# Half of x behind the first weights, rstd on the sums, shift in halves: a reordered start of a fused decoder step on one core

## The chip, the cores and the metric

The kernel runs on one core of a Trainium2 chip. Its metric is the device time of one execution in microseconds (us). The engines are named as in the profile: PE is TensorE (PEld its weight loads), DVE is VectorE, ACT is ScalarE, POOL is GpSimd, and SP is the queue that issues most of the transfers.

## The reference

One step of a one-layer hybrid recurrent decoder trunk in fp32, for 256 prompt tokens and 32 sample tokens (8 sequences of 4), D = 2048. What is cut from it here is the inside of the three mixer branches.

```python
def rmsnorm(x, g):
    y = x * rsqrt(mean(x * x, axis=-1) + EPS)
    return y * g
mod = silu(c) @ w_ada + b_ada                    # c: one row for the prompt, 8 for the samples
sh1, sc1, gt1, sh2, sc2, gt2 = split(mod, 6)
xn = rmsnorm(x, g_norm1) * (1.0 + sc1) + sh1
proj = xn @ w_in                                 # lru_x, q, k, v, gates, ...: 13 groups of columns
...                                              # RG-LRU, GLA and mLSTM branches, merge gates
x = x + gt1 * (merged @ w_out)
xn = rmsnorm(x, g_norm2) * (1.0 + sc2) + sh2
x = x + gt2 * (square(relu(xn @ w_ff1)) @ w_ff2)
y = rmsnorm(x, g_final)
```

## The kernel before

All activations lie feature by partition: 16 tiles (KT) of 128 features by N = 288 tokens, of which the first NP = 256 are the prompt's and the last 32 the samples'. A weight matrix is read in blocks of 512 output columns. `stream` takes a block through PE: for each group of two k tiles it loads 512 KB of weights (`raw`), ScalarE rounds them to `hi`, VectorE forms the rest `lo = raw - hi`, and PE adds three products for each of 4 column tiles and 2 k tiles, `hi*xh + hi*xl + lo*xh`: 24 matmuls of 128x288 a group. `raw`, `hi` and `lo` have three buffers each. A block's four sums lie in PSUM (`mm`, four buffers) and are taken out by `evac`.

The modulation rows (SC1, SH1, ...) come from `w_ada`, which is read in tiles of 1 MB ("units"). `load_one` issues the next unit's load into a slot, and `visit` puts the products of the units that are held on PE (`pa`, line 256). Where both happen is written out by hand: `every("L L L L . V")` gives one token for each group of a stream, L for a load, V for a visit, and a dot for nothing. The loads stand in SP's queue in the order of the program, so an L whose slot isn't free holds back the weight loads behind it. A slot comes free by a visit. The order on PE, DVE, ACT and POOL is made by a scheduler, apart from `issue_after`, which puts an instruction behind another on its engine, and `high_priority`.

The first stretch goes as follows. ScalarE's queue loads x in four pieces, 16 squares are summed by PE (`pi`, line 455) and `rstd_of` makes rstd. `drain("sc0")` takes the eight units of the first half of SC1, and `scale1(0)` forms `x * rstd * sc` for k tiles 0 to 7 and splits it into xh and xl (`modulate`, lines 408 to 438). Blocks 0 to 2 of the projection's q, k and v (NPRE = 3) then run over k tiles 0 to 7 without the shift, `to_slot` takes their sums out (line 465); after the other half of SC1 they run over k tiles 8 to 15, and `plus_slot` adds (line 476). What SH1 gives for these three blocks is added later (`shift_product`, "cor"). For all other blocks `whole` puts xh and xl together again on POOL, `shift` adds SH1 and splits once more (lines 427 to 438), and block 3 starts.

At the end the feed-forward blocks leave x2 in 16 tiles; ScalarE scales tiles 0 to 11 by `g_final` as they come, rstd is made, and the last products (lines 1566 and 1570) and the stores follow.

Of the kernel before, what the change touches and what calls it, by code (L numbers as in the profile page):

```python
# [8 lines left out]
F32 = mybir.dt.float32  # L9
# [5 lines left out]
P = 128  # L15
D = 2048
# [36 lines left out]
def trunk(ctx, tc, io):  # L53
# [91 lines left out]
        at["n"] += 1  # L145
        return [weight_tile(n) for n in ("raw", "hi", "lo")]

    def stream(w, blk, act, kt, evac, g0=0, width=512, ahead=True, k0=0, kg=2):

        nm_t = width // P  # L150
        pss = [pm.tile([P, 512], F32, tag="mm", name=nm("mm")) for _ in range(nm_t)]
        for g in range(k0 // kg, kt // kg):
            with tc.high_priority() if ahead else nullcontext():
                raw, hi, lo = (t.rearrange("p (k m) -> p k m", k=kg) for t in weight_tiles())
                Q.dma_start(raw, w[blk, g0 + g].rearrange("p (k m) -> p k m", k=kg))
                pace["hi"] = S.activation(hi, raw, AF.Copy)  # L156
                pace["lo"] = V.tensor_tensor(out=lo, in0=raw, in1=hi.bitcast(F32), op=ALU.subtract)  # L157
            for m in range(nm_t):
                for kk in range(kg):
                    k = kg * g + kk  # L160
                    xh, xl = act(k)
                    ms = slice(m * P, (m + 1) * P)
                    T.matmul(pss[m][:, :N], hi[:, kk, ms], xh, start=k == k0, stop=False)  # L163
                    T.matmul(pss[m][:, :N], hi[:, kk, ms], xl, start=False, stop=False)  # L164
                    pace["last"] = T.matmul(pss[m][:, :N], lo[:, kk, ms], xh, start=False, stop=k == kt - 1)  # L165
# [173 lines left out]
    left = units()  # L339

    def load_one():
        u = next(left, None)
# [12 lines left out]
    def step(cs):  # L355
        for c in cs:
            if c == "L":
                load_one()
            elif c == "V":
                with tc.high_priority(), tc.issue_after(pace["last"].ins):  # L360
                    visit()

    def drain(n):
        while n not in done:
# [5 lines left out]
    def sumsq(ps, x, k, s):  # L370

        if k == 0:
            S.activation(s, x, AF.Square)
            return
        sq = t288()
        S.activation(sq, x, AF.Square)
# [26 lines left out]
    def smp(a):  # L403
        return a[..., NP:N].rearrange("p k (b t) -> p k b t", b=NB)

    def modulate(xg, rs, k0, fk, xh, xl, xr):

        V.tensor_tensor(out=xr, in0=xg, in1=rs.unsqueeze(1).to_broadcast([P, 4, N]), op=ALU.mult)
        bc = [P, 2, NB, TS]
        for j in range(0, 4, 2):  # L410
            r = slice(k0 + j, k0 + j + 2)
            for i in range(j, j + 2):
                V.tensor_scalar(xr[:, i, 0:NP], xr[:, i, 0:NP], mod[:, fk, k0 + i, 0:1], None, ALU.mult)
            xs = smp(xr[:, j:j + 2])
            G.tensor_tensor(out=xs, in0=xs, in1=mod[:, fk, r, 1:9].unsqueeze(3).to_broadcast(bc), op=ALU.mult)
            split(xh[:, r, :], xl[:, r, :], xr[:, j:j + 2])

    def whole(k0, xh, xl, xr):

        G.tensor_tensor(out=xr, in0=xh[:, k0:k0 + 4, :].bitcast(F32), in1=xl[:, k0:k0 + 4, :].bitcast(F32), op=ALU.add)  # L420

    def shift(k0, shk, xh, xl, xr):

        for j in range(0, 4, 2):
            r = slice(k0 + j, k0 + j + 2)
            for i in range(j, j + 2):
                V.tensor_scalar(xr[:, i, 0:NP], xr[:, i, 0:NP], mod[:, shk, k0 + i, 0:1], None, ALU.add)
            xs = smp(xr[:, j:j + 2])
            V.tensor_tensor(out=xs, in0=xs, in1=mod[:, shk, r, 1:9].unsqueeze(3).to_broadcast([P, 2, NB, TS]), op=ALU.add)
            split(xh[:, r, :], xl[:, r, :], xr[:, j:j + 2])  # L430

    def split(dst_h, dst_l, src):
        n = src.shape[1]
        step = 2 if len(src.shape) == 3 else n
# [8 lines left out]

    xa, xb = slot(0), slot(1)
    xin = halves(xa, xb)
    for i in range(4):
        t = (xa, xb)[i // 2]
        S.dma_start(t[:, 4 * (i % 2):4 * (i % 2) + 4, :], io["x"][:, 4 * i:4 * i + 4, :])
    xh = big.tile([P, KT, N], F32R, tag="xh", name="xh1")
    xl = big.tile([P, KT, N], F32R, tag="xl", name="xl1")  # L450
    ps = longp()
    for k in range(KT):
        sq = t288()
        S.activation(sq, xin(k), AF.Square)
        T.matmul(ps[:, :N], ones, sq, start=k == 0, stop=k == KT - 1)
    rs = rstd_of(ps)

    def act1(k):
        return xh[:, k, :], xl[:, k, :]
# [5 lines left out]
            S.copy(dst[:, base + m, :], p)  # L465
        return f


    slots["ids"] = 2, 4, 5, 6, 7, 8, 9, None
    drain("sc0")  # L470
    xs3, xs4 = slot(3), slot(4)
    qk, vv = slot(8), slot(9)

    def plus_slot(dst, base):
        def f(m, p):
            V.tensor_tensor(out=dst[:, base + m, :], in0=dst[:, base + m, :], in1=p, op=ALU.add)
        return f

    def scale1(h):
        t = (xa, xb)[h]  # L480
        for i in range(2):
            with tc.high_priority():
                modulate(t[:, 4 * i:4 * i + 4, :], rs, 8 * h + 4 * i, SC1, xh, xl, (xs3, xs4)[i % 2][:, 0:4, :])


    slots["ids"] = 2, 5, 6, 7, None
    scale1(0)
# [3 lines left out]
    for b in range(NPRE):  # L491
        run(stream(win, B_Q + b, act1, 8, to_slot((qk, vv)[b // 2], 4 * (b % 2))))
    drain("sc")
    scale1(1)
    for b in range(NPRE):
        run(stream(win, B_Q + b, act1, KT, plus_slot((qk, vv)[b // 2], 4 * (b % 2)), k0=8))
    xrs = [(xs3, xs4)[i % 2][:, 4 * (i // 2):4 * (i // 2) + 4, :] for i in range(4)]
    for i in range(4):
        whole(4 * i, xh, xl, xrs[i])
    drain(SH1)  # L500
    with tc.high_priority():
        for i in range(4):
            shift(4 * i, SH1, xh, xl, xrs[i])
# [121 lines left out]

    ylru = []
    hselr = cp.tile([P, 4], F32R, tag="hselr", name="hselr")
    S.activation(hselr, C("hsel"), AF.Copy)
# [33 lines left out]
    every("L L L L . V . .")  # L662
# [370 lines left out]
    every("L L . V . .")  # L1033
    merge(0, ylru, io["wbl"])


# [388 lines left out]

    merge(1, ygla, io["wbg"])
    slots.update(ids=(None, 8), n=0)
    every("L L . . V . .", skip=5)

    mo = slot(3)  # L1430
    for b in range(2):
# [95 lines left out]
    def ff2(hb, h):  # L1527
        for b in range(4):
            def ev(m, p, b=b):
# [10 lines left out]
                    return  # L1540
                resid(x, p, GT2, k)
                sumsq(pss, x, k, ssum)
                if k < 12:
# [7 lines left out]
    for hb in range(8):  # L1551
# [5 lines left out]
            ssum = row("gc")  # L1557
        ff2(hb, h)
        h = hn
    rs = rstd_of(pss)  # L1560
    for i, (a, b) in enumerate(((0, 2), (8, 10), (2, 5), (10, 12), (5, 8), (12, 14), (14, 16))):
        t = x2[a // 8][:, a % 8:(b - 1) % 8 + 1, :]
        with tc.high_priority():
            if b <= 12:
                E = G if a >= 8 else V
                E.tensor_tensor(out=t, in0=t, in1=rs.unsqueeze(1).to_broadcast([P, b - a, N]), op=ALU.mult)
            else:
                for k in range(a, b):
                    x = x2[1][:, k - 8, :]
# [113 lines left out]
```

## Time and profile before

| | us |
|---|---|
| median of 3 runs (1971.32 to 1976.9) | 1974.94 |
| the profiled execution | 1968.77 |
| its span, first to last instruction | 1967.0 |
| PE busy | 1928.3 |
| DVE busy | 1022.5 |
| ACT busy | 818.1 |
| POOL busy | 223.4 |

The mean granted TensorE clock of that execution is 0.993, and 428.99 MB were moved. In the views below a row of the timeline is: start, length, engine, line, operation, output<-input, form, count, and in brackets the idle time of the engine just before and what ended it. A row of grouped instructions is: line, engine, operation, output<-input, form, count, then busy us and mean ns, then the idle time before them. A row of waits is: who waited, for whom, total us, times, longest. Matmuls are pipelined, and one that stands with 0.29 us starts 0.13 us after the one ahead of it.

### The profile page before, as it was taken

Reading aid. Unit: us, or ns where it says so; the run is one execution under the profiler, and the core shown is the slowest. Engines: PE = TensorE matmul, PEld = TensorE weight load, DVE = VectorE, ACT = ScalarE, POOL = GpSimd, SP = SyncE. Lnnn points to the kernel's source line nnn. Section 1 sums busy time; section 2 is a strip of 40 time slices with the busy share of each in tenths; the row PEclk is TensorE's granted clock in tenths of the full one; section 3 lists DMA queues with packets and bytes.
Section 4 is the critical chain, followed back from the end, with each engine's and each line's share of the span. In section 5 each row is a group of like instructions: output and inputs, shape, how many; then the busy total and the mean of one; then the engine's idle time right before and its main releaser. Section 6 shows DMA issues by size and latency. Waiting matters only on the chain.

```text
span 1967.0 us, 35580 instructions
## 1 busy us (share of the span) xinstructions
PE 1928.3 (98%) x14930; PEld 1819.0 (92%) x14930; DVE 1022.5 (52%) x1512; ACT 818.1 (42%) x1161; POOL 223.4 (11%) x293
## 2 busy tenths in 40 slices
PE   6999999999999999999999999999999999999996
PEld 4879888999999999898999899999999999999996
DVE  3453547545674457654445564445444445454565
ACT  3333365535454354433333453443333334343433
POOL 0300100000123010000013330000000000010102
PEclk8999999999999999999999999999999999999998
DMA  9997765636743359866788554644444444444442
GB/s 382 387 346 275 274 238 221 246 130 247 263 166 134 140 184 324 307 251 238 278 318 330 187 212 170 223 159 170 170 164 160 170 161 161 166 171 168 160 172 102
DMA packets 119377, 428.99 MB, mean 218 GB/s; under 512 B 11744, under 2 KB 11904, under 8 KB 119088
## 3 DMA queue, kind: packets, MB, share of 16 engines
q1 hardware_dynamic: 109600, 391.92, 54.5%
q0 software_dynamic: 4576, 16.57, 2.4%
q10 hardware_dynamic: 5040, 18.22, 2.3%
q8 instruction: 117, 1.92, 0.4%
q14 instruction: 44, 0.36, 0.1%
HBM read 409.85 MB, written 16.81 MB: 217 GB/s over the span
## 4 chain that ended last, share of the span: by engine, by line
PE 90%; DMA 4%; DVE 3%; ACT 1%; issue 1%; SPq 0%; DVEq 0%; ACTq 0%
PE mm L163 27%; PE mm L165 27%; PE mm L164 27%; PE pa L256 4%; DMA raw<-win 3%; DVE lo L157 1%; ACT hi L156 1%; DVE s L513 1%; DMA s<-wada 1%; DMA raw<-wbl 1%; PE px L1343 0%; PE px L594 0%; PE pi L1326 0%; DMA raw<-wbm 0%; PE px L864 0%
## 5 line engine op out<-in xcount | busy, mean ns | idle before, releaser
L157 DVE TENSOR_TENSOR lo<-raw,hi 128x1024 fp32r<-128x1024 f32 x448 | 555.1, 1240 | 618.3 <-ACT hi L156 605.0
L156 ACT ACTIVATE hi<-raw 128x1024 fp32r<-128x1024 f32 x448 | 474.5, 1060 | 804.8 <-PE mm L164 530.3
L163 PE MATMUL mm<-xh,hi 128*128 128x288 f32 x2560 | 755.9, 299 | 9.0 <-ACT xh L437 5.4
L164 PE MATMUL mm<-xl,hi 128*128 128x288 f32 x2560 | 752.0, 296 | 0.0
L165 PE MATMUL mm<-xh,lo 128*128 128x288 f32 x2560 | 732.2, 296 | 1.4 <-DVE lo L157 1.3
L163 PEld LDWEIGHTS mm<-xh,hi 128*128 128x128 f32 x2560 | 479.5, 188 | 32.7 <-issue 13.5
L163 PE MATMUL mm<-s,hi 128*128 128x288 f32 x1664 | 490.0, 297 | 1.6 <-ACT s L1004 1.6
L164 PE MATMUL mm<-s,hi 128*128 128x288 f32 x1664 | 487.9, 295 | 0.0
L164 PEld LDWEIGHTS mm<-xl,hi 128*128 128x128 f32 x2560 | 481.9, 188 | 2.1 <-issue 0.5
L165 PEld LDWEIGHTS mm<-xh,lo 128*128 128x128 f32 x2560 | 474.6, 189 | 5.0 <-DVE lo L157 2.7
L165 PE MATMUL mm<-s,lo 128*128 128x288 f32 x1664 | 475.9, 295 | 0.6 <-DVE lo L157 0.6
L163 PEld LDWEIGHTS mm<-s,hi 128*128 128x128 f32 x1664 | 311.9, 188 | 8.2 <-issue 5.2
L164 PEld LDWEIGHTS mm<-s,hi 128*128 128x128 f32 x1664 | 312.5, 188 | 0.3
L165 PEld LDWEIGHTS mm<-s,lo 128*128 128x128 f32 x1664 | 308.3, 188 | 1.2 <-DVE lo L157 1.1
L157 DVE TENSOR_TENSOR lo<-s,hi 128x1024 fp32r<-128x1024 f32 x80 | 98.0, 1225 | 115.2 <-ACT hi L156 115.2
L156 ACT ACTIVATE hi<-s 128x1024 fp32r<-128x1024 f32 x80 | 84.9, 1061 | 143.2 <-PE mm L164 142.5
L1521 POOL TENSOR_TENSOR t<-t 128x288 f32<-128x288 f32 x64 | 60.2, 951 | 643.0 <-ACT t L1520 643.0
L1537 DVE TENSOR_TENSOR s<-s,mm 128x288 f32<-128x288 f32 x96 | 40.3, 451 | 33.8 <-PE mm L165 32.6
L256 PE MATMUL pa<-s,silc 128*32 128x512 f32 (+1 forms) x488 | 53.1, 521 | 4.6 <-DMA s<-wada 4.6
L438 DVE TENSOR_TENSOR s<-t,s 128x288 fp32r<-128x288 f32 x64 | 33.8, 568 | 15.5 <-ACT s L437 15.5
L1024 POOL TENSOR_TENSOR s<-s,t 128x288 f32<-128x288 f32 x16 | 16.5, 1058 | 192.8 <-DVE t L1023 192.8
L437 ACT ACTIVATE s<-t 128x288 fp32r<-128x288 f32 x64 | 28.0, 441 | 24.6 <-POOL t L1521 24.6
(391 smaller groups left out, 1102.1 us busy)
## 6 DMA issues: line engine op xcount, KB each, us to landing
raw<-win SPq DMA_DIRECT2D x192, 512.0 KB, 5.2
raw<-wf SPq DMA_DIRECT2D x176, 512.0 KB, 4.1
s<-wada SPq DMA_DIRECT2D x48, 1024.0 KB, 8.8
s<-wf SPq DMA_DIRECT2D x80, 512.0 KB, 3.2
ag<-wada SPq DMA_DIRECT2D x30, 1024.0 KB, 5.7
raw<-wout SPq DMA_DIRECT2D x32, 512.0 KB, 5.7
st<-wada SPq DMA_DIRECT2D x24, 512.0 KB, 7.1
s<-win SPq DMA_DIRECT2D x13, 768.0 KB, 6.7
```

The source lines that it names most:

```text
L156: pace["hi"] = S.activation(hi, raw, AF.Copy)
L157: pace["lo"] = V.tensor_tensor(out=lo, in0=raw, in1=hi.bitcast(F32), op=ALU.subtract)
L163: T.matmul(pss[m][:, :N], hi[:, kk, ms], xh, start=k == k0, stop=False)
L164: T.matmul(pss[m][:, :N], hi[:, kk, ms], xl, start=False, stop=False)
L165: pace["last"] = T.matmul(pss[m][:, :N], lo[:, kk, ms], xh, start=False, stop=k == kt - 1)
L256: pace["prod"] = T.matmul(ps[32 * j:32 * j + 32, h * w // 4:(h + 1) * w // 4], stat(k), v[:, j], start=k == 0 and h == 0, stop=k == KT - 1 ...
L437: S.activation(dst_h[:, r], src[:, r], AF.Copy)
L438: V.tensor_tensor(out=dst_l[:, r], in0=src[:, r], in1=dst_h[:, r].bitcast(F32), op=ALU.subtract)
L513: V.scalar_tensor_tensor(y[:, m, s:NP], x[:, m, 0:NP - s], w[:, m, j:j + 1], y[:, m, s:NP], ALU.mult, ALU.add)
L1024: (V if br == 1 else G).tensor_tensor(out=a, in0=a, in1=t, op=ALU.add)
L1521: G.tensor_tensor(out=r, in0=r, in1=r, op=ALU.mult)
L1537: V.tensor_tensor(out=a, in0=a, in1=p, op=ALU.add)
```

## The change

- ScalarE's queue loads only the first half of x. The other half goes into SP's queue in two pieces, by a new token X, behind the first weight groups; a new token N squares it on ScalarE and adds it up on VectorE, and one late matmul ends the sum.
- The eight first sums on PE stand one ahead of each of the eight unit products.
- rstd isn't needed at the start any more: `scale` forms `x * sc` for k tiles 0 to 7 and, later, 8 to 15, and `add_slot` multiplies the finished sums of blocks 0 to 2 by rstd on VectorE (`normalise` puts rstd on x itself, for the other blocks). The prompt columns of xh come from ScalarE with a scale, those of xl from one VectorE operation. The first group's matmuls are ordered: all hi*xh, then hi*xl, then lo*xh.
- `whole` and the old `shift` go. SH1 is made in two halves, and `shift` works on x: k tiles 0 to 7 while the three blocks run, 8 to 15 beside block 3.
- The narrow weights (`wn`) get their own buffer instead of one of the three of `raw`, and load earlier.
- Four patterns of visits have their V one group earlier.
- At the end VectorE makes all the last products, in other pieces; ScalarE scales tiles 12 and 13 too.

```diff
     def stream(..., behind=None):
...
-                pace["lo"] = V.tensor_tensor(out=lo, in0=raw, in1=hi.bitcast(F32), op=ALU.subtract)
+                with tc.issue_after(behind.ins) if behind and g == 0 else nullcontext():
+                    pace["lo"] = V.tensor_tensor(out=lo, in0=raw, in1=hi.bitcast(F32), op=ALU.subtract)
...
+            if behind and g == 0:
+                for i in range(3):
+                    for kk in range(kg):
+                        for m in range(nm_t):
+                            with tc.issue_after(pace["last"].ins) if pace["last"] else nullcontext():
+                                part(m, kk, i)
...
         yield from ada_half("sc", SC1, 1)
-        yield from ada(SH1)
+        yield from ada_half("sh0", SH1, 0)
+        yield from ada_half("sh1", SH1, 1)
...
-    for i in range(4):
-        t = (xa, xb)[i // 2]
-        S.dma_start(t[:, 4 * (i % 2):4 * (i % 2) + 4, :], io["x"][:, 4 * i:4 * i + 4, :])
+    for i in range(2):
+        S.dma_start(xa[:, 4 * i:4 * i + 4, :], io["x"][:, 4 * i:4 * i + 4, :])
...
-    for k in range(KT):
-        sq = t288()
-        S.activation(sq, xin(k), AF.Square)
-        T.matmul(ps[:, :N], ones, sq, start=k == 0, stop=k == KT - 1)
-    rs = rstd_of(ps)
...
+    slots.update(ids=(2, 3, 4, 5, 6, 7, None, 9), n=0)
+    for u in range(8):
+        load_one()
+    for u in range(8):
+        sq = t288()
+        S.activation(sq, xin(u), AF.Square)
+        with tc.issue_after(pace["prod"].ins) if u else nullcontext():
+            pace["sum"] = T.matmul(ps[:, :N], ones, sq, start=u == 0, stop=False)
+        with tc.issue_after(pace["sum"].ins):
+            visit(1)
...
+    def samples(x, r, kind, op):
+        xs, h = x[:, :, NP:N], xh[:, r, NP:N]
+        V.tensor_tensor(out=smp(x), in0=smp(x), in1=mod[:, kind, r, 1:9].unsqueeze(3).to_broadcast([P, 2, NB, TS]), op=op)
+        V.tensor_copy(h, xs)
+        return V.tensor_tensor(out=xl[:, r, NP:N], in0=xs, in1=h.bitcast(F32), op=ALU.subtract)
+    def scale(k, order=None):
...
+            then(samples(x, r, SC1, ALU.mult))
+        for i in range(2):
+            f = mod[:, SC1, k + i, 0:1]
...
+                then(S.activation(xh[:, k + i, 0:NP], x[:, i, 0:NP], AF.Copy, scale=f))
...
+                l = then(V.scalar_tensor_tensor(xl[:, k + i, 0:NP], x[:, i, 0:NP], f, xh[:, k + i, 0:NP].bitcast(F32), ALU.mult, ALU.subtract))
+    def normalise(k):
+        x, r = pair_of(k)
+        for i in range(2):
+            V.scalar_tensor_tensor(x[:, i, 0:NP], x[:, i, 0:NP], mod[:, SC1, k + i, 0:1], rs[:, 0:NP], ALU.mult, ALU.mult)
+        V.tensor_tensor(out=x[:, :, NP:N], in0=x[:, :, NP:N], in1=rs[:, NP:N].unsqueeze(1).to_broadcast([P, 2, NS]), op=ALU.mult)
+    def shift(k):
+        x, r = pair_of(k)
+        samples(x, r, SH1, ALU.add)
+        for i in range(2):
+            f = mod[:, SH1, k + i, 0:1]
+            S.activation(xh[:, k + i, 0:NP], x[:, i, 0:NP], AF.Identity, bias=f)
+            V.scalar_tensor_tensor(xl[:, k + i, 0:NP], x[:, i, 0:NP], f, xh[:, k + i, 0:NP].bitcast(F32), ALU.add, ALU.subtract)
-    def plus_slot(dst, base):
+    def add_slot(dst, base):
         def f(m, p):
-            V.tensor_tensor(out=dst[:, base + m, :], in0=dst[:, base + m, :], in1=p, op=ALU.add)
+            d = dst[:, base + m, :]
+            V.tensor_tensor(out=d, in0=d, in1=p, op=ALU.add)
+            V.tensor_tensor(out=d, in0=d, in1=rs, op=ALU.mult)
...
+    def second_half():
+        while len(sums) < 2:
+            yield
+        with tc.issue_after(pace["last"].ins):
+            T.matmul(ps[:, :N], ones, ssq, start=False, stop=True)
+        inv_sqrt(rs, ps[:, :N], bias=eps, scale=1.0 / D)
...
-    every("L LV " * 4 + "L LLV L LV " * 3 + "LV" + " ." * 40)
+    every(". L X L LV LN XL LV LN LV L L L LV L L LLV L L L LV L L LLV")
...
+    pre = beside(second_half())
+    for h in range(2):
+        for b in range(NPRE):
+            ev = (add_slot if h else to_slot)((qk, vv)[b // 2], 4 * (b % 2))
+            run(stream(win, B_Q + b, act1, 8 + 8 * h, ev, k0=8 * h, behind=None if h or b else ready))
+    finish(pre)
     every("L L L L . V")
...
+    rest = beside(last_shifts())
...
+            wn = sp.tile([P, 1028], F32, tag="st", name=nm("st"), bufs=2)[:, 0:512].rearrange("p (k c) -> p k c", k=KT)
+            Q.dma_start(wn, io["wsm"].rearrange("p (k c) -> p k c", k=KT))
...
-    wn = wp.tile([P, 1024], F32, tag="raw", name=nm("raw"), bufs=3)[:, 0:512].rearrange("p (k c) -> p k c", k=KT)
-    Q.dma_start(wn, io["wsm"].rearrange("p (k c) -> p k c", k=KT))
...
-    every("L L L . V . .", skip=6)
+    every("L L L V . . .", skip=6)
     merge(2, yml, io["wbm"])
...
+        for k in range(12, 14):
+            x = x2[1][:, k - 8, :]
+            S.activation(x, x, AF.Copy, scale=Pm("gf")[:, k:k + 1])
...
-    for i, (a, b) in enumerate(((0, 2), (8, 10), (2, 5), (10, 12), (5, 8), (12, 14), (14, 16))):
+    for i, (a, b) in enumerate(((0, 1), (1, 3), (3, 6), (6, 8), (8, 11), (11, 14), (14, 16))):
...
-            if b <= 12:
-                E = G if a >= 8 else V
-                E.tensor_tensor(out=t, in0=t, in1=rs.unsqueeze(1).to_broadcast([P, b - a, N]), op=ALU.mult)
+            if b <= 14:
+                V.tensor_tensor(out=t, in0=t, in1=rs.unsqueeze(1).to_broadcast([P, b - a, N]), op=ALU.mult)
```

Of the four patterns with an earlier V the one ahead of `merge(2, ...)` is shown; the others are those of the gate blocks, of `merge(0, ...)` and of the two `mo` blocks.

More of the change, by code (lines that the diff above doesn't have):

```diff
@@ L146, in weight_tiles, with stream @@
         return [weight_tile(n) for n in ("raw", "hi", "lo")]
-    def stream(w, blk, act, kt, evac, g0=0, width=512, ahead=True, k0=0, kg=2):
+    def stream(w, blk, act, kt, evac, g0=0, width=512, ahead=True, k0=0, kg=2, behind=None):
         nm_t = width // P
@@ L156, in stream, with part @@
                 pace["hi"] = S.activation(hi, raw, AF.Copy)
-                pace["lo"] = V.tensor_tensor(out=lo, in0=raw, in1=hi.bitcast(F32), op=ALU.subtract)
+                with tc.issue_after(behind.ins) if behind and g == 0 else nullcontext():
+                    pace["lo"] = V.tensor_tensor(out=lo, in0=raw, in1=hi.bitcast(F32), op=ALU.subtract)
+            def part(m, kk, i):
+                k = kg * g + kk
+                ps, ms = pss[m][:, :N], slice(m * P, (m + 1) * P)
+                xh, xl = act(k)
+                w, x = ((hi, xh), (hi, xl), (lo, xh))[i]
+                pace["last"] = T.matmul(ps, w[:, kk, ms], x, start=k == k0 and i == 0, stop=k == kt - 1 and i == 2)
+            if behind and g == 0:
[5 more added lines that the diff above has]
+                yield
+                continue
             for m in range(nm_t):
                 for kk in range(kg):
[L160 to L165, printed above, removed]
+                    for i in range(3):
+                        part(m, kk, i)
                 if g == kt // kg - 1:
@@ L339, in trunk @@
     left = units()
+    also = {}
     def load_one():
@@ L361, in step @@
                     visit()
+            elif c in also:
+                also[c]()
     def drain(n):
@@ L404, in smp @@
         return a[..., NP:N].rearrange("p k (b t) -> p k b t", b=NB)
[L406 to L430, printed above, removed]
     def split(dst_h, dst_l, src):
@@ new lines, in trunk, with pair_of, then, now @@
+    qk, vv = slot(8), slot(9)
+    def pair_of(k):
+        t = (xa, xb)[k // 8]
+        return t[:, k % 8:k % 8 + 2, :], slice(k, k + 2)
+    def samples(x, r, kind, op):
[4 more added lines that the diff above has]
+    def scale(k, order=None):
+        def then(i):
+            if order is not None:
+                order[i.ins.engine] = i
+            return i
+        def now(e):
+            return tc.issue_after(order[e].ins) if order and e in order else nullcontext()
+        x, r = pair_of(k)
+        A, W = mybir.EngineType.Activation, mybir.EngineType.DVE
+        with now(W):
+            then(samples(x, r, SC1, ALU.mult))
+        for i in range(2):
+            f = mod[:, SC1, k + i, 0:1]
+            with now(A):
+                then(S.activation(xh[:, k + i, 0:NP], x[:, i, 0:NP], AF.Copy, scale=f))
+            with now(W):
+                l = then(V.scalar_tensor_tensor(xl[:, k + i, 0:NP], x[:, i, 0:NP], f, xh[:, k + i, 0:NP].bitcast(F32), ALU.mult, ALU.subtract))
+        return l
@@ new lines, in more_x, with norm_part @@
+    def more_x():
+        i = len(xs_)
+        xs_.append(Q.dma_start(xb[:, 4 * i:4 * i + 4, :], io["x"][:, 8 + 4 * i:12 + 4 * i, :]))
+    def norm_part():
+        for k in range(4 * len(sums), 4 * len(sums) + 4):
+            if k == 0:
+                with tc.issue_after(pace["hi"].ins):
+                    S.activation(ssq, xb[:, k, :], AF.Square)
+                continue
+            sq = t288()
+            with tc.issue_after(pace["hi"].ins):
+                S.activation(sq, xb[:, k, :], AF.Square)
+            V.tensor_tensor(out=ssq, in0=ssq, in1=sq, op=ALU.add)
+        sums.append(0)
@@ new lines, in second_half @@
+    def second_half():
+        while len(sums) < 2:
+            yield
+        with tc.issue_after(pace["last"].ins):
+            T.matmul(ps[:, :N], ones, ssq, start=False, stop=True)
+        inv_sqrt(rs, ps[:, :N], bias=eps, scale=1.0 / D)
+        while "sc" not in done:
+            yield
+        for k in range(8, KT, 2):
+            scale(k)
+            yield
+        for k in range(0, KT, 2):
+            normalise(k)
+            yield
+        while "sh0" not in done:
+            yield
+        for k in range(0, 8, 2):
+            shift(k)
+            yield
@@ L488, in trunk, with last_shifts @@
+    def last_shifts():
+        for k in range(8, KT, 2):
+            shift(k)
+            if k != 8:
+                yield
+    xs_, sums = [], []
+    ssq, rs = row("rr"), row("lf")
+    also.update(X=more_x, N=norm_part)
+    slots.update(ids=(2, 3, 4, 5, 6, 7, None), n=0)
+    chain = {}
+    with tc.high_priority():
+        ready = scale(0, chain)
+        for k in range(2, 8, 2):
+            scale(k, chain)
     G.tensor_copy(con[:, 0:1], mod[:, SC1, 0, 0:1])
     G.dma_start(con, io["con"])
-    every("L LV " * 4 + "L LLV L LV " * 3 + "LV" + " ." * 40)
@@ L491, in trunk @@
[L491 to L503, printed above, removed]
+    every(". L X L LV LN XL LV LN LV L L L LV L L LLV L L L LV L L LLV")
@@ L627, in trunk @@
     hselr = cp.tile([P, 4], F32R, tag="hselr", name="hselr")
-    S.activation(hselr, C("hsel"), AF.Copy)
+    with tc.issue_after(pace["hi"].ins):
+        S.activation(hselr, C("hsel"), AF.Copy)
     lx = slot(2)
@@ L660, in gate_silu @@
         return f
-    every("L L L L . V . .")
+    every("L L L L V . . .")
     slots.update(ids=(6, 7, "st", None), n=0)
@@ L1032, in trunk @@
     slots.update(ids=(None, 7), n=0)
-    every("L L . V . .")
+    every("L L V . . .")
     merge(0, ylru, io["wbl"])
@@ L1427, in trunk @@
     slots.update(ids=(None, 8), n=0)
-    every("L L . . V . .", skip=5)
+    every("L L . V . . .", skip=5)
     mo = slot(3)
```

16 lines of the change are left out of this document (4 added, 12 removed).

## The prediction

> **What bounds the kernel now.** The page comes first. Its busy table and its slices say which engine has no time left, and where it still has some.
>
> ```profile
> PE 1928.3 (98%) x14930; PEld 1819.0 (92%) x14930; DVE 1022.5 (52%) x1512; ACT 818.1 (42%) x1161; POOL 223.4 (11%) x293
> ...
> PE   6999999999999999999999999999999999999996
> ```
>
> TensorE (PE) is busy for 98% of the 1967.0 us span; only the first and the last slice show holes. So a change of order can win only what PE does not use: 1967.0 - 1928.3 = 38.7 us, plus stretches where PE is busy at a low clock. The waits of PE say who owns the holes (total, times, longest).
>
> ```profile
> PE pi L455 <- ACT t L454: 6.1, 1, 6.1
> PE mm L163 <- ACT xh L437: 5.4, 1, 5.4
> PE pa L256 <- DMA s<-wada: 4.6, 5, 1.5
> PE mm L163 <- DVE s L476: 2.2, 1, 2.2
> ...
> PE mm L163 <- ACT s L1004: 1.6, 1, 1.6
> ```
>
> The next view is busy time by stretch: length, then PE, PEld, DVE, ACT and POOL busy (instructions), TensorE clock, DMA share, GB/s.
>
> ```profile
> 18.00:22.00 4.00, 2.83 (x36) 1.08 (x34) 2.75 (x5) 0.32 (x1) 0.00 (x0) 1.00 1.02 418
> 22.00:26.00 4.00, 1.79 (x16) 0.59 (x16) 1.05 (x1) 0.00 (x0) 0.00 (x0) 0.65 1.03 417
> 26.00:30.00 4.00, 3.20 (x28) 1.19 (x32) 0.00 (x0) 0.00 (x0) 0.00 (x0) 0.50 1.03 422
> 38.00:42.00 4.00, 3.99 (x16) 3.64 (x16) 4.00 (x6) 2.75 (x4) 0.00 (x0) 0.50 1.03 421
> ...
> 46.00:50.00 4.00, 4.00 (x49) 2.91 (x48) 1.46 (x2) 1.10 (x2) 0.00 (x0) 1.00 1.03 419
> 40.00:120.00 80.00, 79.94 (x663) 65.53 (x662) 35.04 (x41) 25.75 (x35) 16.50 (x10) 0.98 1.00 394
> 70.00:80.00 10.00, 10.00 (x95) 8.91 (x93) 5.43 (x14) 4.93 (x9) 1.32 (x4) 1.00 0.88 343
> 1550.00:1600.00 50.00, 50.00 (x378) 50.00 (x377) 24.93 (x32) 16.99 (x16) 0.00 (x0) 1.00 0.50 178
> ```
>
> Two things bind. The transfers run full until 120 us (share 1.00, 394 GB/s). And PE, once it has its operands, takes 50/378 = 0.132 us a matmul, 3.2 us for a weight group of 24; at clock 0.50 it does 16 in 4 us. The start is read in the timeline (start, length, engine, line).
>
> ```profile
> 31.18 1.07 PE L256 MATMUL pa<-s,silc 128*32 128x256 f32 x16 [0.78 <-DMA s<-wada]
> 32.32 0.45 DVE L219 STREAM_TRANSPOSE t<-pa 128x256 f32<-128x256 f32 x1 [9.27 <-PE pa L256]
> 33.47 1.22 DVE L157 TENSOR_TENSOR lo<-raw,hi 128x1024 fp32r<-128x1024 f32 x1 [0.70 <-ACT hi L156]
> 34.62 0.23 DVE L278 TENSOR_TENSOR mod<-t,par 128x72 f32<-128x72 f32 x1
> 34.88 0.23 DVE L281 SCALAR_TENSOR_TENSOR mod<-mod,par 128x72 f32<-128x72 f32 x1
> 37.66 1.33 PE L163 MATMUL mm<-xh,hi 128*128 128x288 f32 x4 [5.40 <-ACT xh L437]
> 47.14 1.07 PE L256 MATMUL pa<-ag,silc 128*32 128x256 f32 x16
> ...
> 141.53 0.29 PE L165 MATMUL mm<-xh,lo 128*128 128x288 f32 x1
> 144.01 0.37 PE L163 MATMUL mm<-xh,hi 128*128 128x288 f32 x1 [2.19 <-DVE s L476]
> ```
>
> The eighth wada tile lands at 31.18, the first weight matmul starts at 37.66, and two groups (48 matmuls) are through at 47.14: 9.5 us where full clock needs 6.4. From there to 141.5 PE does 22 groups and 24 wada products in 94.4 us without a hole: 22 x 3.2 = 70, so a product costs 1.0 us. Then come 2.3 idle us, and block 3 begins at 144.0.
>
> **Term 1: the first weight matmul comes earlier.** On PE, at the very start (pi: sum of squares of x; pa: wada products; mm: weight matmuls), before:
>
> ```order
> L455 MATMUL pi_108<-t_17_142,ones 128x288
> L256 MATMUL pa_166<-s_27_175,silc 32x256 x8
> L455 MATMUL pi_108<-t_18_145,ones 128x288
> L455 MATMUL pi_108<-t_19_148,ones 128x288
> L455 MATMUL pi_108<-t_20_151,ones 128x288
> L455 MATMUL pi_108<-t_21_154,ones 128x288
> L256 MATMUL pa_166<-s_28_185,silc 32x256 x8
> L256 MATMUL pa_166<-s_29_195,silc 32x256 x8
> ```
>
> and in the change:
>
> ```order
> L460 MATMUL pi_106<-t_19_168,ones 128x288
> L269 MATMUL pa_126<-s_10_115,silc 32x256 x8
> L460 MATMUL pi_106<-t_20_179,ones 128x288
> L269 MATMUL pa_126<-s_11_117,silc 32x256 x8
> L460 MATMUL pi_106<-t_21_190,ones 128x288
> L269 MATMUL pa_126<-ag_119,silc 32x256 x8
> L460 MATMUL pi_106<-t_22_201,ones 128x288
> L269 MATMUL pa_126<-s_13_121,silc 32x256 x8
> L165 MATMUL mm_250<-xh_104,hi_255 128x288
> ```
>
> Eight sums are left, one ahead of each product. Half of x (128 x 2304 floats, 1.18 MB) now loads behind the first weights: at 420 GB/s that is 2.8 us, so the eighth tile lands at 28.4 and its product ends at 29.5. On VectorE (DVE), what stands between that product and xh, before:
>
> ```order
> L219 STREAM_TRANSPOSE t_34_245<-pa_166 128x256
> L157 TENSOR_TENSOR lo_283<-raw_281,hi_282 128x1024
> L278 TENSOR_TENSOR mod<-t_34_245,par 128x72
> L281 SCALAR_TENSOR_TENSOR mod<-mod,par 128x72
> L413 TENSOR_SCALAR s_35_249<-s_35_249,mod 128x256
> ```
>
> and in the change:
>
> ```order
> L232 STREAM_TRANSPOSE t_23_212<-pa_126 128x256
> L291 TENSOR_TENSOR mod<-t_23_212,par 128x72
> L294 SCALAR_TENSOR_TENSOR mod<-mod,par 128x72
> L472 TENSOR_TENSOR s_3_100<-s_3_100,mod 128x2x32
> L473 CAST xh_104<-s_3_100 128x2x32
> L474 TENSOR_TENSOR xl_105<-s_3_100,xh_104 128x2x32
> ```
>
> The lo split has left the path, rstd and its products too; the prompt columns of xh come from ScalarE beside it. The durations of such operations (line, form, count, busy, mean ns):
>
> ```profile
> L429 DVE TENSOR_TENSOR s<-s,mod 128x64 f32<-128x64 f32 x7 | 1.5, 221 | 0.0
> L465 ACT COPY s<-mm 128x288 f32<-128x288 f32 x12 | 4.8, 400 | 16.7 <-PE mm L165 16.1
> L156 ACT ACTIVATE hi<-raw 128x1024 fp32r<-128x1024 f32 x27 | 28.5, 1058 | 59.5 <-DMA raw<-win 45.7 <-PE mm L164 7.1 <-DVE lo L157 3.9
> L476 DVE TENSOR_TENSOR s<-s,mm 128x288 f32<-128x288 f32 x11 | 4.9, 453 | 8.3 <-PE mm L165 7.9
> L157 DVE TENSOR_TENSOR lo<-raw,hi 128x1024 fp32r<-128x1024 f32 x26 | 34.6, 1340 | 34.8 <-ACT hi L156 34.8
> ```
>
> 0.45 + 0.23 + 0.23 + two of 0.22 + gaps of 0.2 = 1.5 us: first matmul at 31.0, 6.7 earlier. ScalarE then has eight scalings queued ahead of the second hi: 8 x 0.40 + 1.06 from 30.6 on ends at 34.9, some 0.7 us after the first group; with the lo behind it I count 1.0 us of stall. At full clock 48 matmuls are through at 31.0 + 6.4 + 1.0 = 38.4 (8.7 gained). At half clock, with 0.7 more for the last product and the old 9.5 us, at 41.2 (5.9 gained). The clock was 1.00 where PE was busy 71% of a stretch (18:22), 0.65 at 45% (22:26), 0.50 later. A sum and a product in each 2.5 us make about 64%, between the first two, so I take the middle: **39.8, a gain of 7.3**. [...]
>
> ```profile
> 26.23 0.20 PEld L256 LDWEIGHTS pa<-s,silc 128*32 128x32 f32 x8 [2.35 <-DMA s<-wada]
> ```
>
> **Term 2: up to block 3.** From 39.8 PE has the same 94.4 us and one late sum (0.55): 134.8. The 2.3 us hole goes, because shift is made by halves: sh0 while groups still run, sh1 behind block 3's first half. What is late next: the splits that VectorE does after each set of products. Behind the sc products the lo of the group after next ends 0.45 + 2 x 0.23 + 6 x 0.22 + 3 x 0.40 + 1.22 = 4.65 us after them, and is wanted a group and 8 matmuls on, at 4.3: 0.35. Behind the sh1 products the next lo ends after 0.45 + 0.23 + 6 x 0.22 + 4 x 0.40 + 1.22 = 4.8: about 0.6. So block 3 starts at **135.7 instead of 144.0: 8.3 us** for terms 1 and 2. rstd costs two adds into one on twelve blocks' sums (12 x 0.45), eight normalisings and a square root inside the stream. They hide under VectorE's idle time (35 busy of 80 us), and the buffer of PSUM comes free after the first add. x's two late loads wait on SP's queue in front of two weight loads; the landings that they wait for are long past.
>
> The cover to watch is the transfers. After the eighth tile 24 groups, 24 tiles and x (12.6 + 25.2 + 1.2 = 39.0 MB) must land before the last four products, at 135.7 - 4 x 1.0 = 131.6. At 394 GB/s they do at 28.4 + 99 = 127.4, 4.2 us early.
>
> **Term 3: visits one group earlier.** The hole behind 144 that this touches, in the timeline: SP stood behind a slot until a visit freed it.
>
> ```profile
> 875.56 0.46 SPq L295 DMA_DIRECT2D s<-wada  x1
> ...
> 891.50 0.33 SPq L155 DMA_DIRECT2D raw<-wbm  x1
> 898.10 0.38 SPq L295 DMA_DIRECT2D ag<-wada  x1
> 906.50 1.06 ACT L156 ACTIVATE hi<-raw 128x1024 fp32r<-128x1024 f32 x1 [8.49 <-DMA raw<-wbm]
> ```
>
> A group (3.2 us) earlier, the 1.6 us wait at 906 goes: **1.5 us**. The last tile of that visit was issued at 875.6, some 20 us before SP went on, so it waits for none. The other patterns meet no wait: nothing. Nor do I count anything for the narrow weights' own buffer.
>
> **Term 4: the end.** VectorE and POOL share the last products; both are slow side by side.
>
> ```profile
> L1566 POOL TENSOR_TENSOR s<-s,row 128x576 f32<-128x576 f32 x2 | 4.1, 2088 | 4.1 <-DVE row L397 4.1
> L1566 DVE TENSOR_TENSOR s<-s,row 128x864 f32<-128x864 f32 x2 | 3.3, 1648 | 0.0
> ...
> 1955.38 2.93 DVE L1566 TENSOR_TENSOR s<-s,row 128x576 f32<-128x576 f32 x2
> ...
> 1959.80 1.04 DVE L1566 TENSOR_TENSOR s<-s,row 128x864 f32<-128x864 f32 x1
> 1960.76 1.36 DVE L1570 SCALAR_TENSOR_TENSOR s<-s,par,row 128x288 f32<-128x288 f32 x3
> ...
> o_y<-s SPq DMA_DIRECT2D x2, 288.0 KB, 2.9
> ```
>
> Alone VectorE took 0.96 for 864 columns (1959.80 to 1960.76) and 0.43 for 288. All of it on VectorE: 0.46 + 3 x 0.96 + 2 x 0.76 + 2 x 0.43 = 5.7, done at 1961.1 instead of 1962.1. The span ended 4.9 us after that, of which 2.9 is a landing and the rest a backlog that should shrink: 1.0 to 2.6, **1.8**. The two scalings that move to ScalarE lie under its wait for the sums.
>
> **Sum.** 8.3 + 1.5 + 1.8 = 11.6 us. The profiled execution took 1968.77 us (span 1967.0), 6 us under the median of the runs shown, so the same off the median: 1974.9 - 11.6 = **1963.3**, rounded 1963.
>
> **The rivals.** *Weights late (0.12).* PE is earlier, the transfers are full as before. For: share 1.00. Against: 4.2 us to spare, PE never waited for a weight there. It decides below 39.0/103.2 = 378 GB/s; at the 343 of 70:80 the last tile lands 10.5 us late, and the time is about 1974; halfway, 1968.
>
> *VectorE becomes the bound: slower (0.08).* In groups 12 to 23 it has 12 lo (16 us), 12 double evictions (11), eight normalisings (9), four shifts (6): 42 of some 54 us. It decides if its queue puts each lo over 1.1 us (8 matmuls) behind its hi: 0.8 us a group and 2.4 at three block changes are 17 us, 5 more than all terms win: 1980. For: the one wait for an eviction, 2.2 us. Against: idle time of 45 us in 80.
>
> *A ceiling on loads (0.03).* If all loads are held to some 360 GB/s, between the 343 of 70:80 and the 378 that suffice, 39.0 MB take 108 us, 5.1 too long: 1968. [...] The rows of 415 to 422 speak against such a ceiling.
>
> *Only the start works (0.05).* If visits and end bring nothing: 1966.6.
>
> **How the numbers follow.** Forecast 0.72, from 1959 (full clock, no backlog, no stall: 15) to 1967. Range 1957 to 1970.5: the cases down to weights half late, and 2 us for the spread of runs. A measurement of this kernel tells 0.3% (5.9 us) from no change. Faster by more: forecast, only-start and half of the weights case, 0.82; within: the rest of it and the ceiling, 0.10; slower 0.08.
>
> **What would show it.** First mm near 31, clock near 1.00 at 31:40, 48 matmuls by 40, block 3 at 136, no wait at 906, VectorE alone after the last rstd. Wrong if PE waits for raw or lo between 45 and 136.

## The result and the profile after

The changed kernel takes 1970.97 us (median of 14 runs, 1969.28 to 1973.05), the kernel before 1971.68 (14 runs, 1969.01 to 1976.9). The ratio is 0.9992, 95% interval 0.9983 to 1.0000: no change that this measurement can tell from none. I had forecast 1963, with a range from 1957 to 1970.5. The profiled execution of the changed kernel took 1971.56 us; its page begins as before's did:

```profile
span 1969.5 us, 35874 instructions
...
PE 1931.1 (98%) x15044; PEld 1820.2 (92%) x15044; DVE 1026.1 (52%) x1576; ACT 823.9 (42%) x1179; POOL 206.4 (10%) x279
```

The start went as planned. The waits of PE in the changed kernel (total, times, longest):

```profile
PE pa L269 <- DMA s<-wada: 5.6, 5, 3.2
PE pi L460 <- ACT t L458: 5.4, 1, 5.4
PE mm L165 <- DVE lo L158: 3.9, 5, 1.4
PE pi L1405 <- DMA s<-mC: 2.6, 1, 2.6
PE pa L269 <- DMA ag<-wada: 2.1, 1, 2.1
PE mm L165 <- ACT xh L493: 1.8, 1, 1.8
PE mm L165 <- DVE s L1099: 1.7, 1, 1.7
```

The 5.4 us wait for xh is 1.8, the 2.2 for a block's sum is gone, and so is the third merge's 1.6. New are 2.6 for s<-mC (a load of the mLSTM state) and more waits for lo. In the timeline and the stretches (length, PE, PEld, DVE, ACT, POOL busy, clock, DMA share, GB/s) the start reads:

```profile
28.53 1.07 PE L269 MATMUL pa<-s,silc 128*32 128x256 f32 x16 [0.69 <-DMA s<-wada]
31.36 2.26 PE L165 MATMUL mm<-xh,hi 128*128 128x288 f32 x8 [1.76 <-ACT xh L493]
...
22.00:26.00 4.00, 1.75 (x18) 0.71 (x18) 0.00 (x0) 0.00 (x0) 0.00 (x0) 1.00 1.03 417
26.00:30.00 4.00, 2.83 (x34) 1.13 (x34) 0.26 (x1) 0.26 (x1) 0.00 (x0) 1.00 1.02 419
31.00:35.00 4.00, 3.63 (x16) 3.67 (x17) 3.84 (x12) 4.00 (x10) 0.58 (x2) 0.57 1.02 407
```

The last product starts at 28.53 (31.18 before) and the first weight matmul at 31.36 (37.66). The clock stays at 1.00 until about 31, then halves for one spell of 3.4 us.

Waits alone do not say where six won microseconds went: PE is busy for 2.8 us more than before. What does say it is a ledger. Every trace holds all 12,672 weight matmuls, 24 to a weight group, in the same group order, so the start of a group in one kernel can be set against its start in another. The table gives, worked out from the traces, the start of a group minus its start in the first profile of the kernel before, in us; minus is earlier, and a row loses time where it rises from one column to the next. The lower rows are runs described further down. In e9 the mLSTM states stand at other groups, so its columns 179 and 190 can't be compared.

| kernel | group 0 | 24 (block 3) | 80 | 88 | 179 | 190 | 211 | last matmul | end |
|---|---|---|---|---|---|---|---|---|---|
| before, time | 37.7 | 144.0 | 367.3 | 400.3 | 780.1 | 826.8 | 903.0 | 1949.9 | 1967.0 |
| changed | -6.3 | -7.1 | -5.9 | +0.3 | +1.7 | +6.2 | +6.3 | +4.4 | +2.5 |
| before, again | -0.1 | -0.4 | -1.1 | -1.1 | -1.3 | +2.7 | +2.7 | +1.6 | +1.6 |
| e1 | -5.8 | -7.2 | -5.0 | -5.0 | -5.1 | -1.0 | -1.0 | -2.9 | -4.7 |
| e2 | -5.5 | -6.9 | -5.2 | -6.1 | -5.0 | -2.2 | -2.1 | -4.0 | -5.9 |
| e3 | 0.0 | -0.9 | +0.6 | +6.7 | +7.7 | +12.5 | +12.5 | +11.7 | +11.7 |
| e4 | -5.6 | -7.0 | -5.5 | -5.5 | -5.5 | -1.8 | -1.8 | -3.4 | -3.2 |
| e6 | +0.2 | -0.3 | +0.8 | +0.8 | +2.0 | +6.8 | +6.8 | +5.5 | +3.6 |
| e7 | -6.6 | -8.0 | -6.2 | -6.2 | -6.2 | -2.4 | -2.4 | -4.0 | -5.9 |
| e8 | -5.5 | -7.9 | -6.5 | -6.5 | -4.9 | -1.9 | -1.9 | -3.8 | -5.6 |
| e9 | -6.3 | -8.6 | -7.3 | -7.3 | -8.8 | -10.9 | -2.1 | -4.0 | -5.8 |

The changed kernel is 5.9 us ahead at group 80 and level at group 88. There, in the first merge, one of its visits stands among full-width transposes (L887). In the rows, 128*128 is a stationary operand of 128 columns, the full width, and 128*32 one of 32. On PE, in the changed kernel:

```profile
379.07 1.04 PE L269 MATMUL pa<-ag,silc 128*32 128x512 f32 x2
380.05 0.33 PE L887 MATMUL px<-con,s 128*128 128x128 f32 x1
380.31 1.05 PE L269 MATMUL pa<-ag,silc 128*32 128x512 f32 x2
381.29 0.33 PE L887 MATMUL px<-con,s 128*128 128x128 f32 x1
...
387.72 1.04 PE L269 MATMUL pa<-s,silc 128*32 128x512 f32 x2
388.70 0.33 PE L887 MATMUL px<-con,s 128*128 128x128 f32 x1
```

Each wada product instruction (two records) is followed by one transpose, eight times over, and each pair takes 1.235 us. This is no wait: PE counts as busy throughout. In the kernel before the same visit stands a group later, beside transposes of 32 columns (L815):

```profile
388.40 1.06 PE L256 MATMUL pa<-ag,silc 128*32 128x512 f32 x8
389.29 1.02 PE L256 MATMUL pa<-s,silc 128*32 128x512 f32 x2
390.14 0.67 PE L815 MATMUL px<-con,s 128*32 128x128 f32 x14
```

### The profile page after: what moved, and what is told of

Its sections match the earlier page's. It is cut to its first block, busy times and chain, and to the rows that moved or that the text cites. A ratio compares the mean times of both kernels' runs of the same rounds, so it can differ in the third digit from the quotient of the medians.

```text
span 1969.5 us, 35874 instructions
## 1 busy us (share of the span) xinstructions
PE 1931.1 (98%) x15044; PEld 1820.2 (92%) x15044; DVE 1026.1 (52%) x1576; ACT 823.9 (42%) x1179; POOL 206.4 (10%) x279
## 4 chain that ended last, share of the span: by engine, by line
PE 93%; DMA 4%; DVE 2%; ACT 1%; issue 1%; DVEq 0%; SPq 0%; ACTq 0%; POOLq 0%
PE mm L165 82%; PE pa L269 5%; DMA raw<-win 2%; DVE lo L158 1%; ACT hi L156 0%; DMA s<-mC 0%; DMA s<-wada 0%; DVE s L591 0%; PE px L672 0%; PE px L1422 0%; PE pi L1405 0%; PE px L943 0%; PE px L1336 0%; DMA o_C_s<-s 0%; PE px L1346 0%
## 5 line engine op out<-in xcount | busy, mean ns | idle before, releaser
L165 PE MATMUL mm<-s,hi 128*128 128x288 f32 x3328 | 660.4, 296 | 0.0
L165 PEld LDWEIGHTS mm<-s,hi 128*128 128x128 f32 x3328 | 529.6, 188 | 5.8 <-issue 5.2
L269 PE MATMUL pa<-s,silc 128*32 128x256 f32 (+1 forms) x624 | 56.1, 452 | 5.6 <-DMA s<-wada 5.6
L1616 DVE TENSOR_TENSOR s<-s,mm 128x288 f32<-128x288 f32 x96 | 40.3, 450 | 33.8 <-PE mm L165 32.6
L269 PEld LDWEIGHTS pa<-s,silc 128*32 128x32 f32 x624 | 19.6, 112 | 26.9 <-issue 12.0
L1103 POOL TENSOR_TENSOR s<-s,t 128x288 f32<-128x288 f32 x16 | 21.0, 1339 | 188.7 <-DVE t L1102 188.7
L395 POOL TENSOR_TENSOR row<-row,t 128x288 f32<-128x288 f32 x24 | 24.9, 1039 | 112.0 <-ACT t L393 111.0
```

The source lines that it names most:

```text
L165: pace["last"] = T.matmul(ps, w[:, kk, ms], x, start=k == k0 and i == 0, stop=k == kt - 1 and i == 2)
L269: pace["prod"] = T.matmul(ps[32 * j:32 * j + 32, h * w // 4:(h + 1) * w // 4], stat(k), v[:, j], start=k == 0 and h == 0, stop=k == KT - 1 ...
L1103: (V if br == 1 else G).tensor_tensor(out=a, in0=a, in1=t, op=ALU.add)
L1616: V.tensor_tensor(out=a, in0=a, in1=p, op=ALU.add)
```

## The experiments

**e1: the first merge's pattern put back.**

```
     slots.update(ids=(None, 7), n=0)
-    every("L L V . . .")
+    every("L L . V . .")
     merge(0, ylru, io["wbl"])
```

> The changed kernel with one of its visit patterns put back: in the first merge the visit stands again one group later. Theory A (the order on PE): the 6.1 us that the changed kernel loses between weight groups 80 and 86 come from eight wada products that stand one by one between eight full-width transposes; put back, they stand beside 32-column transposes, the loss goes, PE is 5.9 us ahead of the kernel before at group 88 instead of 0.3 behind, and the whole takes about 1965. Theory B (the transfers): the earlier start moved the loads, and the loss at this place is a late tile or a slower stretch of PE; the pattern is not its cause, PE is still level with the kernel before at group 88, and the whole stays at 1970 to 1972.

1964.29 us (5 runs); ratio to before 0.9964, 0.9952 to 0.9976. At group 88 it is 5.0 us ahead: nothing is lost between 80 and 88. The visit now stands a group later, beside transposes of 32 columns, like the products themselves:

```profile
383.43 1.07 PE L269 MATMUL pa<-ag,silc 128*32 128x512 f32 x8
384.32 1.02 PE L269 MATMUL pa<-s,silc 128*32 128x512 f32 x2
385.18 0.67 PE L894 MATMUL px<-con,s 128*32 128x128 f32 x14
...
386.07 0.64 PE L269 MATMUL pa<-s,silc 128*32 128x512 f32 x3
```

**e2: the pattern as changed, the products first.**

```
                 p = misc()
-                for i in range(4):
-                    T.transpose(p[:, i * P:(i + 1) * P], ...)
+                with tc.issue_after(pace["prod"].ins):
+                    for i in range(4):
+                        T.transpose(p[:, i * P:(i + 1) * P], ...)
```

> The changed kernel, with every pattern as changed, but the sixteen full-width transposes of vv stand behind the product that is in flight, so that the eight products run together and the transposes after them. Theory A (the alternation itself costs): eight products take about 1.8 us and eight transposes 0.8, 2.6 instead of 9.7; 6 to 7 us go, about 1964.5. Theory B (it is the place, not the alternation: the products are late or slow there whatever stands between them): under 1 us, 1970 to 1972.

1964.44 us; ratio 0.9970, 0.9958 to 0.9982. Same work, same place, another order:

```profile
379.75 1.06 PE L269 MATMUL pa<-ag,silc 128*32 128x512 f32 x8
380.64 1.04 PE L269 MATMUL pa<-s,silc 128*32 128x512 f32 x8
381.61 1.09 PE L888 MATMUL px<-con,s 128*128 128x128 f32 x8
```

Together products and transposes hold up the weight matmuls for 2.79 us, in the changed kernel for 9.80. So it is the alternation that costs, 7.0 us, not the place. The records show what is lost: in e2 four products start within 0.02 us (379.755 to 379.775) and share their time (eight in 0.89 + 0.97 us), while in the changed kernel, with a transpose behind each, each has about 1.0 us to itself (379.07 to 380.05). What in TensorE ends the overlap the traces do not show.

**e3: the kernel before with that pattern alone.**

```
     slots.update(ids=(None, 7), n=0)
-    every("L L . V . .")
+    every("L L V . . .")
```

> The kernel before with only the first merge's pattern changed. Theory A: it loses 6 us at groups 80 to 86 and nothing elsewhere, about 1977.5 where the kernel before takes 1971.7. Theory B (the loss needs the earlier start): no more than 1 us, 1971 to 1973. What I predicted for it blind was nothing.

1978.63 us; ratio 1.0038, 1.0024 to 1.0051. Between groups 80 and 88 it loses 6.1 us, as the changed kernel does: one line of the diff makes the kernel 0.38% slower, with no part in the start.

**e4: the start alone.** The changed kernel with all later edits undone: the four visit patterns, the narrow weights' buffer, the tail.

```
-    every("L L L L V . . .")        (and those of the first and third merge and of the mo blocks)
+    every("L L L L . V . .")
...
-    wn = sp.tile([P, 1028], F32, tag="st", ...)
+    wn = wp.tile([P, 1024], F32, tag="raw", ...)
...
-    for i, (a, b) in enumerate(((0, 1), (1, 3), (3, 6), ...
+    for i, (a, b) in enumerate(((0, 2), (8, 10), (2, 5), ...
```

> The changed kernel's start (x by halves, rstd on the sums, shift by halves, the early visits) with all that comes later as in the kernel before: visit patterns, narrow weights, tail. Theory A: PE is about 7 us ahead at group 24 and about 6 at group 80, keeps it through the merges, and the whole is 4 to 6 us faster than before, 1966 to 1968. Theory B (what the start wins is given back later by waits that were there for slack to absorb, whatever the patterns): ahead at group 24, level by the end, 1970 to 1972.

1965.62 us (10 runs); ratio 0.9971, 0.9961 to 0.9980. Ahead by 7.0 us at group 24 and 5.5 from 80 to 179: the start's gain is carried through the merges.

**The kernel before, again.** All four experiments waited for s<-mC, and the first profile of before did not; so before was profiled a second time.

> The kernel before, unchanged, profiled a second time. In the four experiments so far PE waited 2.2 to 3.3 us for a load of the mLSTM state (s<-mC) near 786, and so did the changed kernel; the profiled execution of the kernel before did not. Theory A (it comes and goes, in the kernel before as well): a second profile shows PE waiting there for 2 us or more, with a span of 1969 to 1971. Theory B (the change and its variants bring it): no such wait, a span near 1967.

One run, 1970.33 us, span 1968.5. Its waits:

```profile
PE mm L163 <- ACT hi L156: 3.4, 3, 2.2
PE pi L1326 <- DMA s<-mC: 2.4, 1, 2.4
...
PE mm L163 <- ACT s L1004: 0.3, 1, 0.3
```

The wait for s<-mC belongs to the kernel before as well: the ledger shows 2.8 to 4.9 us lost between groups 179 and 190 in every profile but the first (e9 aside). And where PE has lost time there, the third merge's wait (ACT s L1004) shrinks, from 1.6 to 0.3 here, 0.7 in e3 and 0.2 in e6. My term 3 was read from the one execution in which it was long. Another loss comes and goes: between groups 88 and 179 the changed kernel, e2, e3, e6 and e8 lose 1.0 to 1.6 us, in a wait for VectorE at group 112, and the other rows but e9 0.1 or less, whatever their edits.

**e6: the kernel before with the new tail alone.**

```
-                if k < 12:
+                if k < KT - 4:
...
-            if b <= 12:
-                E = G if a >= 8 else V
-                E.tensor_tensor(out=t, ...)
+            if b <= 14:
+                V.tensor_tensor(out=t, ...)
```

> The kernel before with only the tail changed (the last sums' scalings on ScalarE, the closing products on VectorE alone, cut in other pieces). My term 4: nothing until the last weight matmul, and the end 1.8 us (1.0 to 2.6) earlier, counted from the last matmul on; about 1969.7 where the kernel before takes 1971.5. Rival (the last store takes it back): the output leaves no earlier, within 0.5 us.

1970.18 us (11 runs); ratio 0.9988, 0.9979 to 0.9997. From the last weight matmul to the end 1.85 us are gone (+5.5 to +3.6 in the ledger), as in the changed kernel. VectorE's closing products, in e6:

```profile
1960.87 1.43 DVE L1569 TENSOR_TENSOR s<-s,row 128x288 f32<-128x288 f32 x2
...
1962.21 0.51 DVE L1573 SCALAR_TENSOR_TENSOR s<-s,par,row 128x288 f32<-128x288 f32 x1
1962.64 3.35 DVE L1569 TENSOR_TENSOR s<-s,row 128x864 f32<-128x864 f32 x4
1965.91 0.51 DVE L1573 SCALAR_TENSOR_TENSOR s<-s,par,row 128x288 f32<-128x288 f32 x1
```

From 1960.87 to 1966.42 is 5.55 us; I had worked out 5.7.

**e7: as e1, and the third merge's old pattern too.**

```
     slots.update(ids=(None, "st", 5), n=0)
-    every("L L L V . . .", skip=6)
+    every("L L L . V . .", skip=6)
```

> The changed kernel with the first merge's old pattern (as in e1) and also the third merge's old pattern. My term 3: the wait of the third merge (PE for ScalarE, at 906 in the kernel before) comes back with 1.5 us between groups 211 and 213, where e1 gained 1.8 there. Rival, from e4, whose pattern is the old one too and which gained 1.8 all the same: the wait depends on how fast three loads land that run at one time, so it is anywhere between 0 and 1.5 with the old pattern; the place shows no firm difference. The whole within 1.5 us of e1 either way.

1963.44 us (4 runs); ratio 0.9960, 0.9946 to 0.9973. Between groups 211 and 213 it gains 1.8 us on the first profile of before with the old pattern, as e1 does with the new: the pattern brings nothing. Here the clock did not fall at the start at all (mean of that execution 0.998, of the changed kernel's 0.996), and the first two groups were through at 38.3, the full-clock figure of term 1 (38.4).

**e8: as e1, the products with rstd later.**

```
             V.tensor_tensor(out=d, in0=d, in1=p, op=ALU.add)
-            V.tensor_tensor(out=d, in0=d, in1=rs, op=ALU.mult)
+            due.append(d)      (multiplied behind the next block's first lo)
```

> As e1, but on the twelve blocks' sums the product with rstd no longer stands right behind each add: it follows a group later, behind the next block's first lo split. Theory A (the stalls of 2.1 us that the changed kernel has between 95 and 118 are VectorE's queue: eight operations of 0.45 us ahead of a lo): two of the three waits go, PE is 8.3 to 8.9 us ahead of the kernel before at group 24 instead of 7.1, and the whole takes about 1963. Theory B (the transfers or ScalarE hold the start): the waits move to hi or raw, still 7.1 at group 24, 1964.3 as e1.

1963.40 us; ratio 0.9959, 0.9947 to 0.9971. From group 2 to 24 the changed kernel, e1, e2, e4 and e7 lose 2.7 us of their lead each, e8 1.7. So 0.9 us of the stalls is the products in VectorE's queue, where theory A said 1.2 to 1.8; waits of 0.36, 0.17 and 0.60 at the same places stay. The whole time can't be told from e1's. What is queued ahead of the lo in the changed kernel:

```profile
96.00 0.98 DVE L517 TENSOR_TENSOR s<-s,mm 128x288 f32<-128x288 f32 x2 [5.64 <-PE mm L165]
96.90 0.45 DVE L518 TENSOR_TENSOR s<-s,row 128x288 f32<-128x288 f32 x1
97.27 0.45 DVE L517 TENSOR_TENSOR s<-s,mm 128x288 f32<-128x288 f32 x1
97.64 0.45 DVE L518 TENSOR_TENSOR s<-s,row 128x288 f32<-128x288 f32 x1
98.00 1.22 DVE L158 TENSOR_TENSOR lo<-raw,hi 128x1024 fp32r<-128x1024 f32 x1
...
99.28 0.40 PE L165 MATMUL mm<-xh,lo 128*128 128x288 f32 x1 [0.93 <-DVE lo L158]
```

**e9: as e8, with the mLSTM states four groups apart and loaded four groups ahead.**

```
         def pair(k):
-            return 5 + 3 * k
+            return 5 + 4 * k
...
-                do(s + i - 3, load, n)
+                do(s + i - 4, load, n)
```

> As e8 (first merge's old pattern, rstd's products late), and the mLSTM states are spaced by four weight groups instead of three, each load issued four groups ahead of its use instead of three. In every profile but the first of the kernel before, PE waits 2.2 to 3.4 us for one of these loads near 786 and then runs 3.4 us at half clock, 2.8 to 5 us in all between groups 179 and 190. Theory A (the load is issued too late: three groups are 9.6 us, and it lands 7 to 9 us after its issue): the wait and the half clock behind it go, 3 to 4 us, about 1960. Theory B (the loads run into a stretch where all transfers together are full): another load is late instead, or a longer tail of the states makes the third merge wait, within 1 us of e8's 1963.4.

1965.33 us; ratio 0.9967, 0.9955 to 0.9979. Theory A failed: the wait for s<-mC is gone, and nothing is won. Theory B is right only in part: other waits stand in its place, but they are for VectorE and not for a load, and the time is 1.9 us above e8's and not within 1 (the intervals of the two overlap). The waits that e8 does not have:

```profile
PE mm L165 <- DVE s L429: 1.1, 1, 1.1
PE px L836 <- DVE s L838: 0.7, 1, 0.7
...
PE px L1435 <- DVE st L1438: 0.5, 1, 0.5
```

From group 160 to 208 PE takes 188.2 us, in e8 186.3. Spread further, the states' matmuls also met a visit: one such place, products alternating with L1418 and L1435, holds the weights up for 3.4 us, their own time included, where the visit at this place takes 1.95 on its own in e8. Where the rest of what the wait had cost went is open. Nor did the half clock that the expectation speaks of stand in every profile: it followed the wait in five of nine (see the last section).

e1, e2, e4, e7, e8 and e9 all beat both kernels, by ratios whose intervals lie below the changed kernel's. Of these e7 and e8 are the fastest, 1963.4, and not to be told from e1.

## Why the prediction was wrong, step by step

**The step that failed is in term 3: "The other patterns meet no wait: nothing."** The pattern of the first merge meets no wait, and costs 6.1 us. I priced a visit by what PE and SP wait for, and never asked what its eight products would stand between on PE. The order of the changed kernel's instructions on PE, which the prediction quotes for the start, would have shown the alternation at this place too. Undone (e1, e2) or put in alone (e3), it moves the time by 6.7, 6.5 and 7.2 us.

**Term 1 was right**: first matmul 31.36 (31.0 forecast), two groups through at 39.28 (39.8), 7.9 us gained where I said 7.3. The middle that I took between the two clocks was a guess that came out: in the seven profiles with this start the clock fell for no spell (e7, e9: group 2 starts at 38.3 and 38.6) or for one (39.1 to 39.4), and the half-clock bound of 41.2 never came.

**Term 2 was mis-sized.** From there to block 3 I counted 95.9 us, of these 0.95 of stalls; it took 97.7, with waits of 0.55, 0.93, 0.16 and 0.98. The hole of 2.2 us went as forecast, but the stalls are not where I put them, behind the sc and sh1 products. The first is for ScalarE's taking out of a block's sums (L450); the other three, 2.1 us, stand behind the second half's sums, where the products with rstd double VectorE's queue ahead of a lo (0.9 of them by e8). Waits for lo between 45 and 136 were a sign of being wrong that I had named. The products' work I had put at nothing ("they hide under VectorE's idle time"). An idle share of half says nothing about a queue that arrives at once. Block 3 starts at 136.95, not 135.7: 7.1 us gained, not 8.3. Of this 1.2 us more is lost by group 80. 0.7 of it falls on groups 24 and 25, where the second half of the shift stands beside block 3, with only 0.15 on record as a wait; the cause of this part is open.

**Term 3's 1.5 us was no gain of the pattern** (e4, e7). **Term 4 was right**: 1.85 measured, 1.8 forecast.

Added up, 7.1 at the start less 1.2 by group 80, less 6.1 in the first merge, and 1.85 at the end leave about 1.6 us of the 11.6 forecast; the medians differ by 0.7.

**The base.** I took the sum off the median of three runs, 1974.94. Over 14 runs it is 1971.68, so the forecast time was 3.3 us too high by its base alone: with the base right, the same sum would have said 1960.1 and missed by more. The first profile of before was also an execution without the wait for s<-mC, and I read its wait at 906 as if every execution had it.

The rivals did not happen. The weights were not late: from the first weight matmul to block 3 PE waits for no hi and no load, and the transfers ran at 412 GB/s from 40 to 80, so nothing held the loads to the 360 GB/s of the third rival. VectorE did not become the bound, though its waits of 2.1 us are 1.1 more than I counted for it. The slower case that I missed was not one of busy engines or transfers, but of order within one engine.

## What to carry to other kernels

Work that is moved to another place in an engine's queue has to be priced with its new neighbours, also when nothing waits there. Here eight narrow matmuls (32 columns of 128) and eight full-width ones held the weights up for 2.79 us as two runs and for 9.80 us one by one in turn. The profile showed this as busy time, so the list of waits did not find it; a ledger of the same instruction's start in both traces did. Keep such matmuls together with an order edge (`issue_after`; e2: 7.0 us for one line). And read a wait as a property of the kernel only if a second profile has it too.

## What the runs showed of the hardware

The alternation is exact: 40.3 us from group 82 to 90 in both kernels that have it, 34.08 in the kernel before and in e1, 33.29 in e2.

Away from the trace's end the clock records hold spells at 0.50 of 6.83 us (from 23.2) and 10.24 us (from 33.4) in the first profile of before, and of 3.41 us (from 31.2 and from 789.0) in the changed kernel. There, around the wait for s<-mC:

```profile
786.00:789.00 3.00, 0.39 (x12) 0.11 (x8) 1.23 (x1) 1.06 (x1) 0.00 (x0) 1.00 1.04 424
789.00:792.00 3.00, 3.00 (x17) 2.20 (x16) 0.87 (x2) 0.38 (x1) 0.53 (x1) 0.50 1.02 419
792.00:796.00 4.00, 4.00 (x31) 4.00 (x30) 1.14 (x4) 1.06 (x1) 0.53 (x1) 0.95 0.95 361
```

Here a wait of 2.6 us is followed by a spell at half clock. In e7 a longer wait for the same load, 3.4 us, ends at 781.8, and the clock holds:

```profile
781.80:784.80 3.00, 3.00 (x27) 2.59 (x28) 2.24 (x5) 0.38 (x1) 0.53 (x1) 1.00 1.04 404
```

Of the nine profiles with this wait five have the spell behind it (changed, before again, e3, e4, e6; waits of 2.2 to 3.3 us; clock 0.50 from 787 to 790 in before again; mean clocks of the executions 0.991 to 0.996) and four do not (e1, e2, e7, e8; 2.4 to 3.4; means 0.997 and 0.998), so the length of the wait does not decide. Between groups 179 and 190 the five lose 1.6 to 1.9 us beyond their wait, the four 0.3 to 0.4 (e1 beyond a second wait of 1.2): a spell costs about 1.2 to 1.5 us more here. After the hole of 2.2 us at 144 the clock held in both profiles of before (1.00 from 145 to 148) and fell in e6 (0.53). Nor did a spell need an idle time of its own length: in the first profile of before the clock was 1.00 from 10 to 23.2 and 0.50 from 23.2 to 30, and the weight loader's longest idle time was 1.90 us in the first stretch and 2.35 us in the second (the PEld row in the prediction). What starts a spell these runs do not show.
